# A one-core log-sum-exp on Trainium2: VectorE sums nearly all rows, and the exit waits for the store last

## The chip, the cores and the metric

The kernel runs on one core of a Trainium2 chip. The metric is the device time of one execution in microseconds, as the median of several runs. A profile of one execution stands beside the times; its span runs from the first to the last instruction of the kernel's own program, and the execution's own time is a little longer than the span.

## The reference

The input `x` is 32 x 512 x 1024 in float32, and the reduction is over the last axis (`axis` is -1):

```python
def reference(x, axis):
    x_max = np.max(x, axis=axis, keepdims=True)
    return (x_max.squeeze(axis) + np.log(np.sum(np.exp(x - x_max), axis=axis))).astype(np.float32)
```

The data are drawn from a standard normal distribution. The kernel leaves the maximum out: it computes log(sum(exp(x))). It reads 67.11 MB and writes 0.07 MB.

## The kernel before

The 16,384 rows of 1024 numbers are laid over 128 partitions, so that each partition holds 128 rows that stand one after another in memory. In what follows "a row" is one such row in all 128 partitions at once: 128 x 1024 numbers, 512 KB. There are 128 of them.

`CHUNKS` cuts the 128 rows into 17 chunks, from 16 rows down to one row at the end. SyncE (SP) issues one load for each chunk (`load`, lines 76 to 87). The chunks land in `ring`, a buffer of 51 rows in SBUF. A chunk whose rows would not fit before the end of the ring starts at slot 0 again. Each load has a semaphore of its own, `landed[i]`. Before a load is issued, SP waits until the slots that it writes have been used: `busy` holds for each slot the count of `act_done` (ScalarE) or of `dve_done` (VectorE) that says so. The first four chunks have 51 rows together and need no wait. The first load is issued before the entry barrier, the others stand in SP's queue in order.

Two engines share the sums. ScalarE (ACT) waits for `landed[i]`. The number beside each chunk's length in `CHUNKS` says how many of its rows VectorE (DVE) will sum. Those rows ACT takes in one instruction, Exp in place (line 116), and DVE adds up each of them with one `reduce_sum` over all of them (line 121). The other rows ACT takes one by one (line 128), with an accumulator output that gives the sum directly; in the profile such a row is an ACTIVATE and an ACTIVATION_READ_ACCUMULATOR. Sums lie in `sums`, one column for each row.

`take_logs` (line 89) waits for the counts of both engines and applies Ln to a range of columns of `sums`. It is called once ahead of chunk `LN_AT` and once at the end. ACT then issues one store of `res`, 128 x 128 numbers. GpSimd (POOL) waits for the store to land (line 141). Then follows the exit that the context emits when it closes, recorded under line 189: a barrier of all engines, GpSimd's clearing of a range of semaphores, and another barrier. In a barrier each engine drains and counts up a semaphore, GpSimd gathers the counts, and then releases the others.

The order on each engine is the order in which the program is written; no scheduler moves anything.

Of the kernel before, what the change touches and what calls it, by code (L numbers as in the profile page):

```python
# [1 line left out]

# [4 lines left out]

CHUNKS = [  # L10
    (4, 1), (15, 11), (16, 10), (16, 15), (16, 0), (14, 0), (12, 9), (9, 5), (7, 5), (5, 4),
    (4, 3), (3, 0), (2, 2), (2, 2), (1, 0), (1, 0), (1, 0),
]
RING_ROWS = 51

LN_AT = 5

FIRST_PARTS = [("sync", 0, 128)]


@with_exitstack
def kernel(
    ctx: ExitStack,
    tc: tile.TileContext,
    x: bass.AP,
    axis: bass.AP,
    out: bass.AP,
):
    nc = tc.nc
    P = nc.NUM_PARTITIONS  # L30

    assert axis in (-1, len(x.shape) - 1), f"only last-axis reduction supported, got {axis}"

    x_flat = x.flatten_outer_dims()
    N, D = x_flat.shape
    assert N % P == 0
    NB = N // P
    assert sum(r for r, _ in CHUNKS) == NB

    fp32 = mybir.dt.float32  # L40
    Exp = mybir.ActivationFunctionType.Exp
    Ln = mybir.ActivationFunctionType.Ln
    AX = mybir.AxisListType.X

    x_v = x_flat.rearrange("(p t) d -> p t d", p=P)
    out_v = bass.AP(tensor=out.tensor, offset=out.offset, ap=[[NB, P], [1, NB]])

    ring = nc.alloc_sbuf_tensor("ring", [P, RING_ROWS, D], fp32).ap()
    sums = nc.alloc_sbuf_tensor("sums", [P, NB], fp32).ap()
    res = nc.alloc_sbuf_tensor("res", [P, NB], fp32).ap()  # L50

    landed = [tc.alloc_semaphore(f"landed{i}") for i in range(len(CHUNKS))]
    act_done = tc.alloc_semaphore("act_done")
    dve_done = tc.alloc_semaphore("dve_done")
    stored = tc.alloc_semaphore("stored")


    hook = nc.pop_inst_callback()
    symbolic, nc._always_lower_symbolic_ap = nc._always_lower_symbolic_ap, False


    place = []
    row = slot = 0
    for r, _ in CHUNKS:
        if slot + r > RING_ROWS:
            slot = 0
        place.append((slot, row))
        slot += r
        row += r

    busy = [(0, 0)] * RING_ROWS
    acts = dves = 0

    def load(i):
        (s, row), r = place[i], CHUNKS[i][0]
        act_wait = max(a for a, _ in busy[s : s + r])
        dve_wait = max(d for _, d in busy[s : s + r])
        if dve_wait:  # L80
            nc.sync.wait_ge(dve_done, dve_wait)
        if act_wait:
            nc.sync.wait_ge(act_done, act_wait)
        for engine, lo, hi in FIRST_PARTS if i == 0 else [("sync", 0, P)]:
            getattr(nc, engine).dma_start(
                out=ring[lo:hi, s : s + r], in_=x_v[lo:hi, row : row + r]
            ).then_inc(landed[i], 16)

    def take_logs(lo, hi, dve_wait, act_wait):
        nonlocal acts  # L90
        nc.scalar.wait_ge(act_done, act_wait)
        nc.scalar.wait_ge(dve_done, dve_wait)
        nc.scalar.activation(out=res[:, lo:hi], in_=sums[:, lo:hi], func=Ln).then_inc(  # L93
            act_done, 1
        )
        acts += 1

    body = nc.main_func.blocks[-1]
    assert not body.instructions
    load(0)  # L100
    n_early = len(body.instructions)

    nc.scalar.preload_act_table_set("natural_log_exp_and_others")  # L103

    logged = 0
    done_before = [(0, 0)]
    for i, (r, n_dve) in enumerate(CHUNKS):
        if i:
            load(i)
        s, row = place[i]  # L110
        if i == LN_AT:
            logged = row
            take_logs(0, logged, *done_before[i])
        nc.scalar.wait_ge(landed[i], 16 * (len(FIRST_PARTS) if i == 0 else 1))
        if n_dve:
            nc.scalar.activation(  # L116
                out=ring[:, s : s + n_dve], in_=ring[:, s : s + n_dve], func=Exp
            ).then_inc(act_done, 1)
            acts += 1
            nc.vector.wait_ge(act_done, acts)  # L120
            nc.vector.reduce_sum(  # L121
                out=sums[:, row : row + n_dve], in_=ring[:, s : s + n_dve], axis=AX
            ).then_inc(dve_done, 1)
            dves += 1
            for j in range(n_dve):
                busy[s + j] = (0, dves)
        for j in range(n_dve, r):
            nc.scalar.activation(  # L128
                out=ring[:, s + j],
                in_=ring[:, s + j],  # L130
                func=Exp,
                accum_out=sums[:, row + j : row + j + 1],
            ).then_inc(act_done, 1)
            acts += 1
            busy[s + j] = (acts, 0)
        done_before.append((dves, acts))

    take_logs(logged, NB, dves, acts)
    nc.scalar.wait_ge(act_done, acts)
    nc.scalar.dma_start(out=out_v, in_=res).then_inc(stored, 16)  # L140
    nc.gpsimd.wait_ge(stored, 16)

    first = nc.main_func.blocks[0]
    head, work = first.instructions, body.instructions
    end = next(k for k, i in enumerate(head) if i.opcode == "UnconditionalBranch")
    head, tail = head[:end], head[end:]
    for ins in work[:n_early]:
        at = next(  # L150
            k for k, i in enumerate(head) if i.engine == ins.engine and i.opcode == "Drain"
        )
        head.insert(at, ins)
    first.instructions = head + work[n_early:] + tail
    body.instructions = []

    nc._always_lower_symbolic_ap = symbolic
    nc.push_inst_callback(hook)


# [1 line left out]
_INS = ['x', 'axis']  # L162
_OUTS = [((32, 512), 'float32')]

_NUMBERS = {'axis': -1}


# [26 lines left out]
```

The softmax here doesn't subtract the row's maximum and nothing guards it: scores larger than these inputs give would overflow.

## Time and profile before

| what | value |
|---|---|
| time, median of 9 runs | 164.24 us (164.08 to 164.49) |
| time of the profiled execution | 164.12 us |
| its span | 162.3 us |
| ACT busy | 124.1 us, 76% of the span |
| DVE busy | 72.9 us, 45% |
| DMA queue of the loads | 67.11 MB, 96.5% of 16 engines' span |
| mean rate over the span | 414 GB/s |
| Exp of whole chunks (L116) | 11 instructions, 59.3 us |
| Exp of single rows with sums (L128) | 61 rows, 63.4 us and 11.3 us of accumulator reads |
| sums on DVE (L121) | 11 instructions, 72.9 us |

Busy time counts the instructions of an engine. Neighbouring instructions overlap a little, so durations of many small ones add up to more than the time that passes. A name such as `128x5120` is partitions by elements of each partition, so 5120 is five rows. Of a load, the profile has the issue on the SP queue and the time until its semaphore has been counted up by all its parts, its landing.

### The profile page before, as it was taken

What the parts mean: (1) busy time and instruction counts of PE and PEld (TensorE: products, weight loads), DVE (VectorE), ACT (ScalarE), POOL (GpSimd) and SP (SyncE); (2) the same over time, 40 slices, a digit from 0 to 9 for tenths busy, and PEclk for the clock granted to TensorE, in tenths of its full rate; (3) what the DMA queues carried; (4) which work ended last, traced back from release to release, by engine and by line L of the source; (5) the groups of instructions that cost most, each with busy time, mean ns of one, the idle gap of its engine ahead of it and who ended that gap; (6) DMA issues with size and microseconds to landing.
All of it is one profiled execution on the core that took longest, in us unless ns stands there. A gap on an engine that the chain in (4) does not pass through costs nothing.

```text
span 162.3 us, 213 instructions
## 1 busy us (share of the span) xinstructions
DVE 72.9 (45%) x11; ACT 124.1 (76%) x136; POOL 0.2 (0%) x4
## 2 busy tenths in 40 slices
DVE  0030000029960799000899900000006999799591
ACT  3180006997089981999339999999999999999993
POOL 0000000000000000000000000000000000000000
DMA  7999889979969969969988999998999999999970
GB/s 262 497 484 469 378 363 517 468 307 517 484 291 517 484 291 517 517 291 484 517 382 384 424 396 444 484 460 388 418 436 408 431 420 419 424 429 417 412 309 16
DMA packets 2593, 67.18 MB, mean 414 GB/s; under 512 B 288, under 2 KB 416, under 8 KB 800
## 3 DMA queue, kind: packets, MB, share of 16 engines
q1 hardware_dynamic: 2448, 67.11, 96.5%
q10 hardware_dynamic: 144, 0.07, 0.1%
q14 instruction: 1, 0.01, 0.0%
HBM read 67.11 MB, written 0.07 MB: 414 GB/s over the span
## 4 chain that ended last, share of the span: by engine, by line
ACT 52%; DMA 38%; DVE 7%; issue 1%
DMA ring<-in_x_dram 38%; ACT ring L128 30%; ACT ring L116 22%; DVE sums L121 7%; ACT res L93 0%
## 5 line engine op out<-in xcount | busy, mean ns | idle before, releaser
L121 DVE TENSOR_REDUCE sums<-ring 128x5 f32<-128x5120 f32 (+8 forms) x11 | 72.9, 6648 | 86.1 <-ACT ring L116 86.0
L116 ACT ACTIVATE ring<-ring 128x5120 f32<-128x5120 f32 (+8 forms) x11 | 59.3, 5393 | 29.6 <-DMA ring<-in_x_dram 29.6
L128 ACT ACTIVATE ring<-ring 128x1024 f32<-128x1024 f32 x61 | 63.4, 1040 | 5.3 <-DMA ring<-in_x_dram 5.3
L128 ACT ACTIVATION_READ_ACCUMULATOR ring<-ring 128x1 f32 x61 | 11.3, 186 | 0.0
L103 ACT ACT_TABLE_LOAD x1 | 1.3, 1283 | 0.8 <-PEq L175 0.8
L93 ACT ACTIVATE res<-sums 128x67 f32<-128x67 f32 (+1 forms) x2 | 0.5, 256 | 0.1
L175 POOL MEMSET const-bfloat16-1.0<- 128x1 bf16 x1 | 0.1, 102 | 0.0
L175 POOL MEMSET const-uint8-127<- 128x1 uint8 x1 | 0.1, 102 | 0.0
L175 POOL MEMSET const-float32-0.0<- 128x1 f32 x1 | 0.1, 99 | 0.2 <-issue 0.2
L175 POOL MEMSET const-float32-1.0<- 128x1 f32 x1 | 0.1, 99 | 0.0
## 6 DMA issues: line engine op xcount, KB each, us to landing
ring<-in_x_dram SPq DMA_DIRECT2D x1, 7680.0 KB, 25.0
ring<-in_x_dram SPq DMA_DIRECT2D x1, 7168.0 KB, 36.1
ring<-in_x_dram SPq DMA_DIRECT2D x1, 6144.0 KB, 21.6
ring<-in_x_dram SPq DMA_DIRECT2D x1, 4608.0 KB, 32.1
ring<-in_x_dram SPq DMA_DIRECT2D x2, 2048.0 KB, 26.3
ring<-in_x_dram SPq DMA_DIRECT2D x1, 3584.0 KB, 40.2
ring<-in_x_dram SPq DMA_DIRECT2D x1, 2560.0 KB, 44.4
ring<-in_x_dram SPq DMA_DIRECT2D x2, 1024.0 KB, 46.0
```

The lines of the kernel that those rows point to most:

```text
L93: nc.scalar.activation(out=res[:, lo:hi], in_=sums[:, lo:hi], func=Ln).then_inc(act_done, 1)
L103: nc.scalar.preload_act_table_set("natural_log_exp_and_others")
L116: nc.scalar.activation(out=ring[:, s : s + n_dve], in_=ring[:, s : s + n_dve], func=Exp).then_inc(act_done, 1)
L121: nc.vector.reduce_sum(out=sums[:, row : row + n_dve], in_=ring[:, s : s + n_dve], axis=AX).then_inc(dve_done, 1)
L128: nc.scalar.activation(out=ring[:, s + j], in_=ring[:, s + j], func=Exp, accum_out=sums[:, row + j : row + j + 1],).then_inc(act_done, 1)
L175: nc = _bacc.Bacc("TRN2", target_bir_lowering=False, num_devices=1)
```

## The change

It has two parts.

First the exit. The semaphores are taken from the core object and not from the tile context, so the context does not clear them. ACT clears `landed`, `act_done` and `dve_done` right after it has issued the store. The context is closed inside the kernel, so that its exit barriers are emitted there. Only behind them does GpSimd wait for the store, and it counts the semaphore `stored` back to zero in the same instruction.

Second the sums. A chunk in `CHUNKS` now has four entries: its rows, the rows that DVE sums, the number of parts into which these are cut (each part is one Exp and one sum), and whether DVE sums them by halves. By halves means one `tensor_tensor_reduce` for each row: it adds the second 512 numbers to the first 512 and accumulates the results, written in the program's order of instructions as a pass of 128x512 and a read of the accumulator. DVE sums 119 rows, of them 16 by halves, where it summed 67; ACT sums 9 rows with its accumulator, where it summed 61. The number of chunks stays 17: the chunk of 12 has one row more, and one of the two chunks of 2 has become a chunk of 1. The first four chunks are as long as before and still fill the ring with 51 rows. The chunk of 9 now starts at slot 0, because the 13 rows ahead of it leave only 8 slots.

The last four rows have their sums in PSUM (`late`). Ln is taken three times: over 81 columns ahead of chunk 7, over 43 columns ahead of the last chunk, and over the 4 columns of `late` at the end.

```diff
 CHUNKS = [
-    (4, 1), (15, 11), (16, 10), (16, 15), (16, 0), (14, 0), (12, 9), (9, 5), (7, 5), (5, 4),
-    (4, 3), (3, 0), (2, 2), (2, 2), (1, 0), (1, 0), (1, 0),
+    (4, 4, 1, False), (15, 15, 1, False), (16, 16, 2, False), (16, 16, 2, False),
+    (16, 15, 2, False), (14, 14, 2, False), (13, 12, 2, False), (9, 8, 1, False),
+    (7, 7, 1, True), (5, 4, 1, True), (4, 3, 1, True), (3, 3, 1, False), (2, 2, 1, True),
+    (1, 0, 1, False), (1, 0, 1, False), (1, 0, 1, False), (1, 0, 1, False),
 ]
-LN_AT = 5
+LN_AT = 7
+LN_LAG = 1
+LATE = 4
...
+    late = nc.alloc_psum_tensor("late", [P, 512], fp32).ap()
...
-    landed = [tc.alloc_semaphore(f"landed{i}") for i in range(len(CHUNKS))]
-    act_done = tc.alloc_semaphore("act_done")
-    dve_done = tc.alloc_semaphore("dve_done")
-    stored = tc.alloc_semaphore("stored")
+    landed = [nc.alloc_semaphore(f"landed{i}") for i in range(len(CHUNKS))]
+    act_done = nc.alloc_semaphore("act_done")
+    dve_done = nc.alloc_semaphore("dve_done")
+    stored = nc.alloc_semaphore("stored")
+    used = sorted(sem.num for sem in [*landed, act_done, dve_done])
...
+    def cuts(n, parts):
+        ends = [-(-n * k // parts) for k in range(parts + 1)]
+        return [(lo, hi) for lo, hi in zip(ends, ends[1:]) if lo < hi]
...
+    late_row = place[-LATE][1]
+    def total(t):
+        return late[:, t - late_row : t - late_row + 1] if t >= late_row else sums[:, t : t + 1]
...
         if i == LN_AT:
-            logged = row
-            take_logs(0, logged, *done_before[i])
+            logged = place[i - LN_LAG][1]
+            take_logs(0, logged, sums[:, :logged], *done_before[i - LN_LAG])
+        if i == len(CHUNKS) - 1:
+            take_logs(logged, late_row, sums[:, logged:late_row], *done_before[-LATE])
...
-        if n_dve:
+        for lo, hi in cuts(n_dve, parts):
             nc.scalar.activation(
-                out=ring[:, s : s + n_dve], in_=ring[:, s : s + n_dve], func=Exp
+                out=ring[:, s + lo : s + hi], in_=ring[:, s + lo : s + hi], func=Exp
             ).then_inc(act_done, 1)
             acts += 1
             nc.vector.wait_ge(act_done, acts)
-            nc.vector.reduce_sum(
-                out=sums[:, row : row + n_dve], in_=ring[:, s : s + n_dve], axis=AX
-            ).then_inc(dve_done, 1)
...
+            if by_halves:
+                for j in range(lo, hi):
+                    nc.vector.tensor_tensor_reduce(
+                        out=ring[:, s + j, : D // 2],
+                        in0=ring[:, s + j, : D // 2],
+                        in1=ring[:, s + j, D // 2 :],
+                        scale=1.0,
+                        scalar=0.0,
+                        op0=Add,
+                        op1=Add,
+                        accum_out=sums[:, row + j : row + j + 1],
+                    ).then_inc(dve_done, 1)
...
+            else:
+                nc.vector.reduce_sum(
+                    out=sums[:, row + lo : row + hi], in_=ring[:, s + lo : s + hi], axis=AX
+                ).then_inc(dve_done, 1)
...
         for j in range(n_dve, r):
             nc.scalar.activation(
                 out=ring[:, s + j],
                 in_=ring[:, s + j],
                 func=Exp,
-                accum_out=sums[:, row + j : row + j + 1],
+                accum_out=total(row + j),
             ).then_inc(act_done, 1)
...
-    take_logs(logged, NB, dves, acts)
+    take_logs(late_row, NB, late[:, : NB - late_row], dves, acts)
     nc.scalar.wait_ge(act_done, acts)
     nc.scalar.dma_start(out=out_v, in_=res).then_inc(stored, 16)
-    nc.gpsimd.wait_ge(stored, 16)
+    nc.scalar.sem_clear(range(used[0], used[-1] + 1))
...
     nc._always_lower_symbolic_ap = symbolic
     nc.push_inst_callback(hook)
+    tc.close()
+    tc.compile()
+    nc.gpsimd.wait_ge(stored, 16)
+    nc.gpsimd.sem_inc(stored, -16)
```

## The prediction

> **What bounds the kernel now.** I read the bar of the page first, then the DMA queues, the timeline of ScalarE (ACT) and VectorE (DVE), the landing times, and last the exit (line 189). The first fence is the page: the chain by engine and the load queue. The second is the timeline: start, duration, engine, line, operation, and in brackets the idle time before it. The third is the last load: its issue in the timeline of the SP queue, and its size and us to landing in the DMA view of that moment.
>
> ```profile
> DMA  7999889979969969969988999998999999999970
> ACT 52%; DMA 38%; DVE 7%; issue 1%
> q1 hardware_dynamic: 2448, 67.11, 96.5%
> ```
>
> ```profile
> 83.84 1.06 ACT L128 ACTIVATE ring<-ring 128x1024 f32<-128x1024 f32 x1 [5.30 <-DMA ring<-in_x_dram]
> ...
> 158.34 1.04 ACT L128 ACTIVATE ring<-ring 128x1024 f32<-128x1024 f32 x1
> 159.29 0.19 ACT L128 ACTIVATION_READ_ACCUMULATOR ring<-ring 128x1 f32 x1
> 159.51 0.25 ACT L93 ACTIVATE res<-sums 128x61 f32<-128x61 f32 x1
> 159.79 0.37 ACTq L140 DMA_DIRECT2D out_dram<-res  x1
> ```
>
> ```profile
> 112.45 0.45 SPq L85 DMA_DIRECT2D ring<-in_x_dram  x1
> ...
> ring<-in_x_dram SPq DMA_DIRECT2D x1, 512.0 KB, 45.8
> ```
>
> The chain gives ACT 52%, but that is a backlog that ends by itself: ACT waited for rows 52 to 67 until 83.84, and the last load, issued at 112.45, lands 45.8 later, at 158.25. ACT starts that row at 158.34, 0.1 behind it. The load stream (96.5% of the DMA engines, one row of 128x1024 in (158.25 - 83.84) / 61 = 1.22 us) therefore sets 158.25, whatever ACT has to spare before. After it come one row, Ln, store and exit. The exit, from the view of line 189 (count, duration in ns, first and last start):
>
> ```profile
> out_dram<-res ACTq DMA_DIRECT2D x1, 64.0 KB, 1.6
> L189 POOLq COMPARE_BRANCH  x1: 33/33/33, 161.4 to 161.4; - x1
> L189 POOLq EVENT_SEMAPHORE  x4: 17/17/17, 161.6 to 162.2; - x4
> L189 POOLq EVENT_SEMAPHORE_RANGE_CLEAR  x1: 139/139/139, 161.9 to 161.9; - x1
> ```
>
> The store lands at 159.79 + 1.6 = 161.4. Only then does GpSimd pass its branch and run two barriers with the clearing between them, to 162.3: 0.9 us in which nothing else runs. The run took 164.12 us, so 1.8 us lie outside the span; the median of the runs is 164.24.
>
> [...] The 64 KB store needs 1.6 us from issue to landing: [...] so about 1.2 us after its 0.37 us of issue are free for other work. [...]
>
> **Prices.** From the rows: TENSOR_REDUCE 16152 ns for 15 rows and 1220 for one give 1.067 us per row + 0.15; two back to back at 123.28 take 15.14 against 9.75 + 5.48, so 0.09 overlaps and the step is 1.067n + 0.06. A chunk's Exp takes 0.853n + 0.20, and its neighbour follows after 0.853n + 0.10 (9 rows: 115.39 to 123.16). A row with accumulator takes 1.04. DVE starts 0.03 after Exp ends.
>
> **The change part by part.**
>
> *Rows moved from ACT to DVE.* ACT had 67 whole-chunk rows and 61 with accumulator; now 119 and 9. 52 rows times (1.04 - 0.85) is some 9 us less ACT work, worth nothing by itself: the loads cover it.
>
> *Supply of loads.* Ring slots now come free by DVE. The load of rows 52 to 67 goes out when the 15-row reduction is done: Exp 25.78 to 38.8, reduction to 55.0 (before: 47.3). Its data are not due until the earlier load has landed at 64.5: 9 us to spare. The next go out at about 72 and 81 (due 84 and 101). The 13-row chunk makes the 9-row one wrap to slot 0, behind the second part of the 16-row chunk: about 107, due 116.5. Later ones have 20 us. So SP's longer waits cost nothing, and the last landing stays at 158.25; one more single-row load adds 0.05 at most.
>
> *DVE at the end.* This is the part that decides. Landings (old issue plus old time to landing, shifted by the rows moved): chunk of 13 at 116.5, 9 at 127.5, 7 at 136.0, 5 at 142.05, 4 at 147.0, 3 at 150.7, 2 at 153.2, singles at 154.4, 155.7, 157.0, 158.3. DVE runs without a break from 90.9 (first half of the 16 rows of 83.84): 8.59 + 7.52 x 3 + 6.46 x 2 = 44.1, to 135.0. ACT on the 13-row chunk: 116.5 + 5.22 + 5.22 + 1.04 + 0.2 for the early Ln = 128.2, and its 8-row Exp is done at 135.2. DVE takes those 8 rows to 143.9, then 16 rows by halves, t us each, with the whole 3-row reduction (3.26) among them and 0.1 to drain. **DVE is done at 147.3 + 16t.** ACT reaches the Ln of these rows at 150.7 + 2.66 + 1.81 + 3.12 = 158.3. So t above 0.69 makes ACT wait, and each 0.1 us more costs 1.6 us. Queued behind that waiting Ln are the last row, the last Ln and the store.
>
> What is t? [...] If each overlaps its neighbour by the 0.09 of reductions, t = 0.66. Hidden reads give 0.60; no overlap at all 0.85; [...] I take 0.66, because ACT shows this very pattern: its 1.04 step is 0.08 more than the bare Exp step, so an accumulator read there overlaps. Then DVE is done at 157.9, 0.4 before it is wanted.
>
> *Ln split, last sums in PSUM.* The big Ln (43 columns) stands ahead of the last row, which starts at 158.3 + 0.2 = 158.5 instead of 158.34; no wait hides that. The last Ln is for 4 columns: 0.25 - 57 x 0.83 ns = 0.21. The store is issued at 158.5 + 1.17 + 0.21 + 0.03 = 159.9, against 159.79: **+0.1**. Writing and reading PSUM is not in the trace: I give it 0, with -0.1 to +0.1 for the range. Lands at 161.5.
>
> *Exit.* The clearing (0.14 us, the row above) moves to ACT behind the store's issue; the barriers run while the store is in flight. ACT: 159.9 + 0.37 + 0.14 + 0.2 of drain = 160.6; the two barriers took 0.9 with the clearing and the branch, so at most 0.7 without: 161.3, covered by the landing at 161.5 with 0.2 left. If that cover were gone, the excess would be added. Then one wait on GpSimd with its decrement (0.03) and nothing behind it: **-0.9**.
>
> Sum: +0.1 - 0.9 = -0.8, so 164.12 - 0.8 = 163.3 on the profiled execution, and 164.24 - 0.8 = **163.4** on the median. A measurement of this kernel can tell about 0.2%, 0.33 us.
>
> **The rivals.** *The half sums are serial* (t = 0.85): [...] against it, ACT's overlap. DVE is done at 160.9, the wait on it 2.6 us, the result 163.4 + 2.6 = 166.0, slower. The turning point: t = 0.69 + 0.8 / 16 = 0.74; below it the exit still wins. [...] *The exit gains nothing*: the 1.8 us outside the span might contain work that waited for the first of the engines and now waits for GpSimd alone, or the barriers outlast the store; then 0.1 us is lost and it is 164.3. For it, no row outside the span is shown; against it, all engines ended within 0.1 of each other before and the last one sets the end in either case.
>
> **How the numbers follow.** The forecast, t up to 0.72 with the exit's gain: 0.67; its own range 162.9 to 163.8. No gain at the exit, or t between 0.72 and 0.76: 0.08. Serial, or otherwise between 0.76 and 0.9: 0.14. [...] Something smaller that lets time outside the span shrink as well (engines that finish early, under 162.7): 0.03, also faster. Faster 0.70, same 0.08, slower 0.22. The range from 162.7 to 166.1 holds the first three cases and leaves out about 0.11.
>
> **What would show it.** Right: the last single-row load lands at 158.2 to 158.4; the last Ln on 43 columns starts without waiting on DVE; the pass of 128x512 near 690 ns with a step of 0.66; no exit rows after the store's landing but GpSimd's wait; span 161.5. Wrong: ACT idle before the 43-column Ln, released by DVE; a pass of 1.2 us; or a last landing beyond 158.6, which would mean that the ring held up a load (the 9-row one first).

## The result and the profile after

| | before | after |
|---|---|---|
| median | 164.24 us (31 runs) | 163.12 us (10 runs) |
| ratio, 95% interval | | 0.9931 (0.9923 to 0.9939) |
| profiled execution, its span | 164.12, 162.3 us | 163.25, 161.4 us |

The change makes the kernel faster by 1.13 us (0.69%; the interval is 1.00 to 1.26 us). The forecast was 0.8: the right way, and 0.3 short.

The page of after: the busy bar of each engine, and the chain.

```profile
DVE  0028000004999999999999599999999999999892
DMA  7999799979989999889989999999999999999990
...
q1 hardware_dynamic: 2448, 67.11, 97.0%
...
DMA 49%; DVE 29%; ACT 20%; issue 0%
```

From the tenth slice on DVE is busy nearly all the time; its longest break there is a wait of 1.9 us for ACT, near 90 us. In the chain ACT's share has fallen from 52% to 20%, and DVE's has risen from 7% to 29%. But the loads still fill 97% of the DMA engines (96.5% before). Which of the two sets the end is read in the last microseconds. The timeline of after, with rows left out where dots stand (start, duration, engine, line, operation, in brackets the idle time before):

```profile
152.57 0.08 DVE L141 DVE_READ_ACCUMULATOR2_ANT sums<- 128x1 f32 x1
153.61 3.35 DVE L154 TENSOR_REDUCE sums<-ring 128x3 f32<-128x3072 f32 x1 [0.95 <-ACT ring L134]
...
156.28 1.04 ACT L161 ACTIVATE ring<-ring 128x1024 f32<-128x1024 f32 x1
...
157.28 1.05 ACT L161 ACTIVATE ring<-ring 128x1024 f32<-128x1024 f32 x1
...
158.10 0.08 DVE L141 DVE_READ_ACCUMULATOR2_ANT sums<- 128x1 f32 x1
158.23 0.17 ACT L161 ACTIVATION_READ_ACCUMULATOR ring<-ring 128x1 f32 x1
158.28 0.24 ACT L105 ACTIVATE res<-sums 128x43 f32<-128x43 f32 x1
158.43 1.04 ACT L161 ACTIVATE ring<-ring 128x1024 f32<-128x1024 f32 x1
159.37 0.16 ACT L161 ACTIVATION_READ_ACCUMULATOR ring<-ring 128x1 f32 x1
159.56 0.17 ACT L105 ACTIVATE res<-late 128x4 f32<-128x4 f32 x1
159.76 0.37 ACTq L173 DMA_DIRECT2D out_dram<-res  x1
```

And the last load of after, its issue and then its size and time to landing:

```profile
130.22 0.49 SPq L97 DMA_DIRECT2D ring<-in_x_dram  x1
...
ring<-in_x_dram SPq DMA_DIRECT2D x1, 512.0 KB, 28.1
```

It lands at 130.22 + 28.1 = 158.3. DVE's last sum is ready at 158.18, the Ln over 43 columns follows at 158.28 on ACT's own pace, and the last row at 158.43, 0.1 behind its landing. ACT has no idle time at any of these steps. It had none in before either, where the row ahead starts exactly one step of 1.04 before the last one (158.34):

```profile
157.30 1.04 ACT L128 ACTIVATE ring<-ring 128x1024 f32<-128x1024 f32 x1
```

So in both kernels loads and ACT arrive within 0.1 us of each other. It is the loads that allow no earlier start: ACT is busy for 115.1 us in after and for 124.1 in before, and these 9 us less of work have not brought the last row forward. The store is issued at 159.76, where before had 159.79: nearly nothing has moved up to here. What differs comes behind it. The store's landing and the exit rows of after, from the DMA view and the views of lines 176, 196 (the barriers) and 198 (the wait):

```profile
out_dram<-res ACTq DMA_DIRECT2D x1, 64.0 KB, 1.6
...
L176 ACTq EVENT_SEMAPHORE_RANGE_CLEAR  x1: 119/119/119, 160.2 to 160.2; - x1
...
L196 POOLq EVENT_SEMAPHORE  x4: 17/17/17, 160.4 to 160.8; - x4
...
L198 POOLq EVENT_SEMAPHORE  x1: 17/17/17, 161.4 to 161.4; - x1
```

ACT clears right behind the store's issue, which is through at 159.76 + 0.37 = 160.13. The four steps of GpSimd's two barriers lie between 160.4 and 160.8, half a microsecond ahead of the store's landing at 159.76 + 1.6 = 161.4. One event of 17 ns at 161.4 is all that is left behind it.

### The profile page after: what moved, and what is told of

Same layout as the page of the kernel before. It is cut to its first block, busy times and chain, and to the rows that moved or that the text cites. A ratio compares the mean times of both kernels' runs of the same rounds, so it can differ in the third digit from the quotient of the medians.

```text
span 161.4 us, 149 instructions
## 1 busy us (share of the span) xinstructions
DVE 121.0 (75%) x46; ACT 115.1 (71%) x40; POOL 0.2 (0%) x4
## 4 chain that ended last, share of the span: by engine, by line
DMA 49%; DVE 29%; ACT 20%; issue 0%
DMA ring<-in_x_dram 49%; DVE sums L154 29%; ACT ring L134 17%; ACT ring L161 3%; ACT res L105 0%
## 5 line engine op out<-in xcount | busy, mean ns | idle before, releaser
L154 DVE TENSOR_REDUCE sums<-ring 128x8 f32<-128x8192 f32 (+5 forms) x14 | 111.2, 7995 | 37.2 <-ACT ring L134 37.1
L134 ACT ACTIVATE ring<-ring 128x8192 f32<-128x8192 f32 (+6 forms) x18 | 104.4, 5835 | 43.9 <-DMA ring<-in_x_dram 43.8
L141 DVE CUSTOM_DVE_ANT_0 ring<-ring 128x512 f32<-128x512 f32 x16 | 9.9, 687 | 0.0
L161 ACT ACTIVATE ring<-ring 128x1024 f32<-128x1024 f32 x9 | 9.3, 1041 | 0.0
L161 ACT ACTIVATION_READ_ACCUMULATOR ring<-ring 128x1 f32 x9 | 1.6, 173 | 0.0
L141 DVE DVE_READ_ACCUMULATOR2_ANT sums<- 128x1 f32 x16 | 1.3, 83 | 0.0
L105 ACT ACTIVATE res<-sums 128x81 f32<-128x81 f32 (+1 forms) x2 | 0.5, 248 | 0.0
```

Source lines behind the costliest of these rows:

```text
L105: nc.scalar.activation(out=res[:, lo:hi], in_=src, func=Ln).then_inc(act_done, 1)
L134: nc.scalar.activation(out=ring[:, s + lo : s + hi], in_=ring[:, s + lo : s + hi], func=Exp).then_inc(act_done, 1)
L141: nc.vector.tensor_tensor_reduce(out=ring[:, s + j, : D // 2], in0=ring[:, s + j, : D // 2], in1=ring[:, s + j, D // 2 :], scale=1.0, scal ...
L154: nc.vector.reduce_sum(out=sums[:, row + lo : row + hi], in_=ring[:, s + lo : s + hi], axis=AX).then_inc(dve_done, 1)
L161: nc.scalar.activation(out=ring[:, s + j], in_=ring[:, s + j], func=Exp, accum_out=total(row + j),).then_inc(act_done, 1)
```

## The experiments

Each kernel was timed beside runs of before, whose median was 164.31 us for the first four kernels and 164.03 for the other three. Differences from before are taken from the ratio to those runs; a difference from after is that plus 1.13. Of each kernel one execution is traced, and in these traces the last load lands between 157.9 and 158.6. So a point of time in one trace says less than the distance between two points in it.

**One part alone.** The first kernel has the chunks and sums of before and the exit of after:

```diff
-    landed = [tc.alloc_semaphore(f"landed{i}") for i in range(len(CHUNKS))]
+    landed = [nc.alloc_semaphore(f"landed{i}") for i in range(len(CHUNKS))]
...
-    nc.gpsimd.wait_ge(stored, 16)
+    nc.scalar.sem_clear(range(used[0], used[-1] + 1))
...
+    tc.close()
+    tc.compile()
+    nc.gpsimd.wait_ge(stored, 16)
+    nc.gpsimd.sem_inc(stored, -16)
```

> The chunks and sums of before with the exit of after. Theory (the gain is the exit): the store still lands near 161.4 and nothing but GpSimd's wait comes behind it, so the time falls by the 0.93 us of exit, to 163.3 (163.1 to 163.5). Rival (the gain comes from the sums on VectorE, and what the exit loses comes back outside the span): 164.2, no change from before.

Measured: 163.34 us, ratio 0.9945 (0.9933 to 0.9957), which is 0.90 us (0.71 to 1.10) less than before. In its timeline the last steps of ACT:

```profile
158.54 1.04 ACT L130 ACTIVATE ring<-ring 128x1024 f32<-128x1024 f32 x1
159.49 0.19 ACT L130 ACTIVATION_READ_ACCUMULATOR ring<-ring 128x1 f32 x1
159.71 0.25 ACT L95 ACTIVATE res<-sums 128x61 f32<-128x61 f32 x1
159.99 0.37 ACTq L142 DMA_DIRECT2D out_dram<-res  x1
```

The store is issued 1.45 us after the last row's start, exactly as in before (158.34 to 159.79), and the span ends at 161.6, 1.6 after the issue. The exit alone gives most of the gain: its rival is refuted.

The second kernel is the counterpart, the rows of after with the exit of before:

```diff
-    nc.scalar.sem_clear(range(used[0], used[-1] + 1))
+    nc.gpsimd.wait_ge(stored, 16)
...
-    tc.close()
-    tc.compile()
-    nc.gpsimd.wait_ge(stored, 16)
-    nc.gpsimd.sem_inc(stored, -16)
```

> The chunks and sums of after with the exit of before. Theory: the last load lands at 158.2 to 158.4 and the store is issued at 159.8 as in both kernels, so the time is that of before, 164.2 (163.9 to 164.4). Rival (the gain comes from the sums): 163.1 to 163.4.

Measured: 164.06 us, ratio 0.9985 (0.9978 to 0.9991): 0.25 us less than before (0.15 to 0.36). Small, but not the nothing that my theory had; the rival's 0.8 to 1.1 is refuted. From the timeline of this kernel:

```profile
158.20 1.04 ACT L159 ACTIVATE ring<-ring 128x1024 f32<-128x1024 f32 x1
159.15 0.15 ACT L159 ACTIVATION_READ_ACCUMULATOR ring<-ring 128x1 f32 x1
159.33 0.17 ACT L103 ACTIVATE res<-late 128x4 f32<-128x4 f32 x1
159.53 0.37 ACTq L171 DMA_DIRECT2D out_dram<-res  x1
```

From the last row's start to the store it is 1.33 here and 1.45 in before: the read of the accumulator 0.15 for 0.19, the last Ln 0.17 for 0.25. That is 0.12 of the 0.25. From the last landing to the store it is 1.37 here (landing at 129.96 + 28.2 = 158.16) and 1.39 in the next kernel, which has the same rows, against 1.54 in before and in the first kernel; so up to 0.17 is seen, with landings known to 0.05. Where the rest lies is not shown. The two parts add up: 0.90 + 0.25 = 1.15, against 1.13 for both together.

**The exit split.** After, with the wait put back ahead of the barriers and the clearing left on ACT:

```diff
     nc.scalar.sem_clear(range(used[0], used[-1] + 1))
+    nc.gpsimd.wait_ge(stored, 16)
+    nc.gpsimd.sem_inc(stored, -16)
...
     tc.close()
     tc.compile()
-    nc.gpsimd.wait_ge(stored, 16)
-    nc.gpsimd.sem_inc(stored, -16)
```

> After, with GpSimd's wait for the store put back ahead of the exit barriers; the clearing stays on ScalarE behind the store. It splits the exit's gain. Theory: the branch (0.15) and two barriers (0.33 each by the trace of after) come back behind the landing, the clearing (0.14 and its drains) doesn't: time after + 0.65, 163.6 to 163.9. Rival (the clearing on GpSimd was the larger part): within 0.3 of after, 163.1 to 163.4.

Measured: 163.77 us, ratio 0.9966 (0.9958 to 0.9974), 0.56 us less than before and so 0.57 more than after. The views of lines 178 (wait) and 198 (barriers) of this kernel:

```profile
L178 POOLq EVENT_SEMAPHORE  x1: 17/17/17, 161.5 to 161.5; - x1
...
L198 POOLq EVENT_SEMAPHORE  x4: 17/17/17, 161.6 to 162.1; - x4
```

The barriers are the same four steps in the same half microsecond, only behind the landing at 161.5. So about two thirds of the exit's gain (0.57 of 0.90) is the place of the wait. The rest goes with the clearing on ACT and with the branch, which I expected to come back and which does not stand among this kernel's rows; these two were not taken apart.

**Is VectorE's end in the way?** It was done only 0.1 us before the Ln that needs it. This kernel gives it air:

```diff
-    (7, 7, 1, True), (5, 4, 1, True), (4, 3, 1, True), (3, 3, 1, False), (2, 2, 1, True),
+    (7, 7, 1, True), (5, 4, 1, True), (4, 3, 1, True), (3, 3, 1, True), (2, 2, 1, True),
```

> After, with the chunk of 3 summed by halves too. In after VectorE idles 0.95 us for that chunk's Exp, sums it whole in 3.35, and is done at 158.18, 0.1 ahead of the Ln on 43 columns at 158.28. Theory (the last landing and ScalarE set the end, the sums only have to be in time): 3 x 0.61 = 1.84 in place of 3.35, VectorE done at 156.7, the Ln still at 158.2 to 158.3, time as after, 163.1 within 0.2. Rival (the Ln was held by VectorE's last sums): the Ln and everything behind it come earlier by up to 0.2, span under 161.1, time 162.9.

Measured: 163.31 us, ratio 0.9938 (0.9925 to 0.9951), not to be told from after. From its timeline, DVE's last row and ACT's next steps:

```profile
156.88 0.08 DVE L141 DVE_READ_ACCUMULATOR2_ANT sums<- 128x1 f32 x1
...
158.48 0.24 ACT L105 ACTIVATE res<-sums 128x43 f32<-128x43 f32 x1
158.61 1.05 ACT L161 ACTIVATE ring<-ring 128x1024 f32<-128x1024 f32 x1
```

DVE is done at 156.96, 1.5 us ahead of the Ln, and the Ln doesn't come earlier. (It stands 0.2 later than in after, and so does the last landing, at 130.38 + 28.2 = 158.6.) In after, the sums were in time, if barely.

The next kernel takes the halves away:

```diff
-    (7, 7, 1, True), (5, 4, 1, True), (4, 3, 1, True), (3, 3, 1, False), (2, 2, 1, True),
+    (7, 7, 1, False), (5, 4, 1, False), (4, 3, 1, False), (3, 3, 1, False), (2, 2, 1, False),
```

> After, with no chunk summed by halves: 7, 4, 3, 3 and 2 rows each in one TENSOR_REDUCE. Theory (1.067 us per row plus 0.06 for each): from 144.0 VectorE needs 7.53 + 4.33 + 3.26 + 3.26 + 2.19 + 0.1 = 20.7, done at 164.7 in place of 158.2; ScalarE idles 6.4 ahead of the Ln on 43 columns, released by VectorE, and last row, Ln and store follow it: 163.1 + 6.4 = 169.5 (169.0 to 170.0). Rival (the halves are a convenience, the end is the loads'): within 0.5 of after.

Measured: 169.28 us, ratio 1.0316 (1.0301 to 1.0332). That is 5.2 us more than before, and so 6.3 more than after. Its waits (engine, line, whom it waited for: total, times, longest) and the Ln in its timeline:

```profile
ACT res L105 <- DVE sums L154: 6.3, 1, 6.3
```

```profile
164.27 0.24 ACT L105 ACTIVATE res<-sums 128x43 f32<-128x43 f32 x1 [6.34 <-DVE sums L154]
164.41 1.04 ACT L161 ACTIVATE ring<-ring 128x1024 f32<-128x1024 f32 x1
```

The wait that after doesn't have is there, at the instruction named, and its 6.34 us are the whole loss, within the error. Moving the rows to DVE in whole chunks up to the end would have been slower than before.

**Whole chunks in the middle.** The same end of VectorE, made late in another way:

```diff
-    (4, 4, 1, False), (15, 15, 1, False), (16, 16, 2, False), (16, 16, 2, False),
-    (16, 15, 2, False), (14, 14, 2, False), (13, 12, 2, False), (9, 8, 1, False),
+    (4, 4, 1, False), (15, 15, 1, False), (16, 16, 1, False), (16, 16, 1, False),
+    (16, 15, 1, False), (14, 14, 1, False), (13, 12, 1, False), (9, 8, 1, False),
```

> After, with the five chunks of 16, 16, 16, 14 and 13 rows each taken in one Exp and one sum. Theory: VectorE gets the first rows of the chunk that lands at 84.0 only when all 15 are done, at 97.0, not 91.1, and then runs without a break: 16.05 + 15.0 + 12.9 + 8.6 = 149.6 ahead of the halves in place of 144.0; 14 x 0.61, 3.26 and 2 x 0.61 follow: done at 162.8, 4.6 later than in after. The loads are still in time (the one of 9 rows is issued at 113, due at 116.7). Time 163.1 + 4.6 = 167.7 (167 to 168.4). Rival (what hurts is the ring: loads issued late leave the queue empty): last landing beyond 159 and DMA share under 95% somewhere after 100.

Measured: 167.38 us, ratio 1.0202 (1.0186 to 1.0219), 3.3 more than before and so 4.4 more than after. Its last load, issue and time to landing, and its largest waits of ACT for DVE:

```profile
141.98 0.43 SPq L97 DMA_DIRECT2D ring<-in_x_dram  x1
...
ring<-in_x_dram SPq DMA_DIRECT2D x1, 512.0 KB, 16.4
```

```profile
ACT res L105 <- DVE sums L141: 3.9, 1, 3.9
```

The last row lands at 158.4, close to after's 158.3, although it was issued 12 us later; the load of 9 rows was issued at 112.77. From 100 to 157 us the loads fill 98% of the DMA engines. So the later issues cost no time, and the rival falls. Nearly all of the loss is ACT's wait. Where DVE lost its time, first in after, then in this kernel:

```profile
91.11 52.98 DVE L154 TENSOR_REDUCE sums<-ring 128x8 f32<-128x8192 f32 x7 [1.90 <-ACT ring L134]
```

```profile
96.59 52.64 DVE L154 TENSOR_REDUCE sums<-ring 128x15 f32<-128x15360 f32 x4 [1.28 <-ACT ring L134]
149.14 0.68 DVE L141 CUSTOM_DVE_ANT_0 ring<-ring 128x512 f32<-128x512 f32 x1
...
162.19 0.08 DVE L141 DVE_READ_ACCUMULATOR2_ANT sums<- 128x1 f32 x1
```

DVE starts these sums 5.5 us later than in after, comes to the halves 5.1 later (149.14 for 144.00), and is done 4.1 later (162.27 for 158.18); the last microsecond is the 0.95 of idle time that after has at the chunk of 3. An Exp cut in two costs ACT 0.1 us (12 rows take 10.54 in after and 10.44 here), but it lets DVE start half a chunk earlier, and a DVE that works without a break hands a late start on to its end, less the idle time that it would have met.

**The Ln and PSUM.** After, with all sums in SBUF and one last Ln:

```diff
-        if i == len(CHUNKS) - 1:
-            take_logs(logged, late_row, sums[:, logged:late_row], *done_before[-LATE])
...
-                accum_out=total(row + j),
+                accum_out=sums[:, row + j : row + j + 1],
...
-    take_logs(late_row, NB, late[:, : NB - late_row], dves, acts)
+    take_logs(logged, NB, sums[:, logged:], dves, acts)
```

> After, with the sums of the last four rows in SBUF and one Ln over 47 columns at the end, none ahead of the last row. My prediction put the split at +0.1 and PSUM at 0. If that is right the last row starts at landing + 0.02 to 0.05 and the store is issued within 0.1 of 159.7; time within 0.2 of after. If the PSUM operands are worth more than the split costs, the accumulator read is 186 ns again (156 in after), the Ln 0.24 (0.173), and the store comes 0.05 to 0.1 later than in after.

Measured: 162.92 us, ratio 0.9924 (0.9907 to 0.9941), the same as after within the intervals. Its last load is issued at 129.86 and needs 28.2; its timeline:

```profile
157.03 1.04 ACT L159 ACTIVATE ring<-ring 128x1024 f32<-128x1024 f32 x1
...
158.07 1.04 ACT L159 ACTIVATE ring<-ring 128x1024 f32<-128x1024 f32 x1
159.02 0.19 ACT L159 ACTIVATION_READ_ACCUMULATOR ring<-ring 128x1 f32 x1
159.24 0.24 ACT L105 ACTIVATE res<-sums 128x47 f32<-128x47 f32 x1
159.51 0.37 ACTq L171 DMA_DIRECT2D out_dram<-res  x1
```

The last row starts on its landing (158.06) and one step of 1.04 behind the row ahead: loads and ACT tie here too. The rest takes 1.44, where after needs 1.33. So the split Ln and PSUM save 0.11 behind the start of the last row, and together they delay that start by up to 0.1. With PSUM the rows ahead follow each other at 1.00 (156.28, 157.28) and not at 1.04, which over three rows nearly pays for the 0.15 that the early Ln takes. What is left is too small for a time to show, so which of my two cases holds stays open; the sums in PSUM are not where after's gain comes from. No run pointed to a version that would beat after clearly.

## Why the prediction was right

- *What bounds.* Right. The last landing is at 158.3 in before (158.25 as the views give it) and in after, and the experiments that leave DVE in time all start ACT's last row within 0.2 of its landing. One thing was read too easily: that ACT's backlog ends by itself. In before no idle time of ACT stands in the timeline behind 83.84, so ACT was busy to the end as well and came in level with the loads. That work taken off ACT gains nearly nothing is shown by the result, not by that reading.
- *Supply of loads.* Right. The issues were forecast to move from 47 to 55 and so on, with 9 us to spare; the chain of after has the load at 54.87 and the last landing hasn't moved. The kernel without cuts spent more than half of what was to spare, and its last landing didn't move either.
- *DVE at the end.* The mechanism is right: the two kernels that make DVE late pay for the delay in full (6.3 us measured for 6.4 expected, 4.4 for 4.6). The price t was forecast as 0.66, among cases from 0.60 up. It was my estimate: no row of before shows a pass over two operands. The prices from the rows of before lead to the same estimate, if a pass goes by its 512 elements: half of a row's 1.067 us and the fixed 0.15 of a TENSOR_REDUCE make 0.69, a read at the same 0.15 and two overlaps of 0.09 make 0.66. The pass took 687 ns (690 forecast), and the step is 144.61 - 144.00 = 0.61:

```profile
144.00 0.68 DVE L141 CUSTOM_DVE_ANT_0 ring<-ring 128x512 f32<-128x512 f32 x1
144.61 0.08 DVE L141 DVE_READ_ACCUMULATOR2_ANT sums<- 128x1 f32 x1
144.61 0.69 DVE L141 CUSTOM_DVE_ANT_0 ring<-ring 128x512 f32<-128x512 f32 x1
```

  The read takes 83 ns, not 0.15 us, and the next pass starts with it. It costs no time of its own: of the cases listed this is the one with hidden reads, 0.60, and not the 0.66 that I took. The serial case (0.85) and the pass of 1.2 us are refuted for this operation by these three lines. To the pass of 1.2 us the forecast gave 0.08 of its 0.22 for slower, though no row of before showed one.
- *The margin of DVE.* Wrong in one term. With t = 0.61 my formula 147.3 + 16t gives 157.1, and DVE was done at 158.18. The formula lets DVE run without a break. In fact the quicker halves made it catch up: it waited 0.95 for the Exp of the chunk of 3, which ends at 153.6, and then 3.26 + 2 x 0.61 + 0.08 follow. By an estimate from these times, below a t of about 0.68 (with 144.0 + 14t + 0.1 at 153.6) only the two rows behind that chunk still count for DVE's end (2t and not 16t); the rest is that Exp and that whole reduction. The margin was 0.1, not the 0.4 that I wrote. With the true t my formula was 1.1 us too early, and that DVE was still in time was luck; the kernel with that chunk by halves has 1.5 us to spare.
- *Ln split, last sums in PSUM.* Mis-sized, with the wrong sign: +0.1 was forecast. From the last landing to the store's issue it is 159.79 - 158.25 = 1.54 in before and 159.76 - 158.32 = 1.44 in after, and the time of the rows alone is 0.25 (0.15 to 0.36) below before. I added 0.2 for the Ln ahead of the last row; its step is 0.15, part of it in front of the landing, because the last row lands 0.04 after the Ln begins. And PSUM, which I gave 0, takes some 0.03 off each read (186 ns in before, 150 to 170 in after) and 0.04 off each row's step (1.04 and 1.00), and the last Ln over 4 columns takes 0.17, not 0.21. These reasons may not account for all of it. In the kernel with neither the split nor PSUM the store still comes 159.51 - 158.06 = 1.45 after the landing, so a part of the 0.25 seems to go with the rows moved off ACT, for which I had given nothing; no run takes this apart.
- *Exit.* Right in its size within the span: from the landing to the end it is 0.9 in before and less than 0.1 in after. The cover is larger than forecast, half a microsecond instead of 0.2: the barriers begin at 160.4, not at 160.6, and take 0.5 without the clearing, where I had allowed 0.7. The trace shows the store's 1.6 us from issue to landing, but not what they are spent on. A tenth comes back outside the span: the runs with the wait at the very end (after and the kernels with its exit) lie 1.83 to 1.92 above their spans, those with the wait ahead of the barriers 1.73 to 1.83. What causes it lies outside of what the trace shows. The rival by which the whole gain is given back there had the right place, but measured 0.1 where it had 0.9.

The sum by measured terms: -0.9 for the exit, +0.1 outside of the span, -0.1 to -0.25 for the rows: -0.9 to -1.05, against a fall of 1.13 (1.00 to 1.26) measured. The 0.3 by which the forecast fell short is the term of the rows, +0.1 in the forecast.

## What to carry to other kernels

When loads set the end, look at what stands behind the last one, instruction by instruction: here 0.9 us of exit work could run while the store was under way, and that was four fifths of the gain, while all that was done to the sums (52 rows moved from one engine to another, the halves, PSUM and the split Ln) gave a quarter of a microsecond. An engine that is given more work near the end needs a ledger of its finishing time, chunk by chunk, with the waits on its producer in it; here 0.1 us was left, and 16 rows summed in the ordinary way would have cost six. Cutting a chunk lets the second engine start earlier, and as long as that engine has no idle time the start carries on to its end: here 5.5 us at the start were 4.1 at the end.

## What the runs showed of the hardware that was not expected

- A read of VectorE's accumulator (83 ns) lies beside the next pass, which starts with it (144.61): 16 sums of two 512-element halves go at 0.61 us each, against 1.067 for a row in a TENSOR_REDUCE of many rows.
- ACT's accumulator read is 186 ns into SBUF and 150 to 170 ns into PSUM, the step from row to row is 1.04 us and 1.00, and an Ln over 4 columns of PSUM takes 173 ns.
- In these runs an execution takes 0.1 us more outside its span (1.83 to 1.92 against 1.73 to 1.83) when GpSimd finishes alone, 0.5 us behind the others. The cause is not shown.
